# Products of neighbouring MLP units interleaved: a unit's first product stands between the fifth and sixth of its predecessor

## The chip, the cores and the metric

The kernel runs on one core of a Trainium2 chip. The metric is the device time of one execution in microseconds; the time before is the median of three runs. The core's engines are TensorE (PE), VectorE (DVE), ScalarE (ACT), GpSimd (POOL) and SyncE (SP); transfers are issued by SP, ACT and POOL.

## The reference

One layer of an encoder trunk on 512 tokens of width 2048, in float32:

```python
h = x + stick_breaking_mixer(rms_norm(x, norm_mix), w_qkv, w_o)   # 16 heads of 128
h = h + square(relu(rms_norm(h, norm_mlp) @ w1)) @ w2             # d_ff = 8192
return rms_norm(h, final_norm)
```

The change touches the MLP alone: `w1` is 2048 x 8192, `w2` is 8192 x 2048.

## The kernel before

**Precision.** Every float32 operand is split into two parts, hi (a cast to float32r) and lo (the remainder), and each product is made of three matmuls: hi·hi, hi·lo and lo·hi (`mm3`, lines 148 to 150).

**Units.** The MLP is done in 32 units (`units2`). Units 0 to 15 are the first stage: each makes 512 of the 8192 hidden columns. Units 16 to 31 are the second stage: pairs (c, q), c from 0 to 7, q from 0 to 1, that add 1024 hidden columns' share into one half of the 2048 output columns. Every unit splits its operands into 2 x 2 blocks and does them with seven block products instead of eight (a Strassen-like scheme). `ORDER` (line 385) lists the seven; an entry gives the activation mix on the left, the chain of weights on the right, the PSUM accumulator, and what is added to the chain afterwards:

```python
    ORDER = (
        ("11", "a", "x", (0, 1)),
        ("12", "c", "z", None),
        ("s1", "a", "y", "b"),
        ("s4", "b", "y", (0, 1)),
        ("s2", "a", "x", "c"),
        ("s3", "b", "x", None),
        ("22", "a", "x", None),
    )
```

Here the products are counted from 0 (11) to 6 (22). A chain is a pair of 0.5 MB buffers (tags `ra`, `rb`, `raw`) that holds one block of the weights and is changed in place: after product 0 another block is added to chain a by an accumulating transfer that POOL issues (`nc.gpsimd.dma_start(..., accum_op=ALU.add)`, line 432), after product 2 VectorE adds chain b into a (line 430), after product 3 POOL adds a block to b (line 432), after product 4 VectorE adds c into a.

**Splitting.** `split2` (line 416) goes through all products in order. For each half of a chain ScalarE casts it to hi (`whi`, line 426) and VectorE subtracts to get lo (`wlo`, line 427), into a pool of six buffers; a product uses four. Then come the additions above. It is called one product ahead of `run2`. It also issues the plain fetches (`fetch`, line 403, on SP's queue, line 408) of the next unit: chain a at product 0, c at product 4, b at product 5.

**Running.** `run2` (line 446) does a product's 48 (first stage, 256 columns) or 24 (second stage, 512 columns) matmuls, in two halves s = 0 and 1 with an accumulator bank each, then its evacuation: in the first stage copies, adds, ReLU and squares into tiles whose seven mixes are stored to DRAM (`a_dram`); in the second one VectorE instruction a half that adds the scaled product into a tile of h (line 537). Accumulator x is opened by product 0 and used again by 4, 5 and 6. Bank pool `acc_a` has four banks, two a unit. Small tasks in the list `side` (mixes, stores, reloads) are taken in turn, one after each half.

**Joints.** At the start of the MLP, transposes and mixes of the attention's output are still being done while product 0 of unit 0 runs; the pool `acc_b` then takes over PSUM banks that the transposes used. During unit 15 the mixes of c = 0 (`load_a(0, ...)`, 28 transfers of 256 KB) and the residual h (`load_h`, 16 of 256 KB, line 564) are loaded on SP's queue; in every q = 1 unit the mixes of the next c are queued, a name per product.

**Order.** The framework's scheduler orders each engine's instructions by program order as priority and by its own model of when each is ready; engines run their queues in that order and wait on semaphores.

Of the kernel before, what the change touches and what calls it, by code (L numbers as in the profile page):

```python
# [18 lines left out]
DF = 8192  # L19
# [3 lines left out]
W = 512  # L23
# [17 lines left out]
def trunk_kernel(  # L41
# [18 lines left out]
    acc_a = ctx.enter_context(tc.tile_pool(name="acc_a", bufs=4, space=PSUM))  # L60
# [91 lines left out]
    def ahead(i):  # L152
        split(i + 1)
        load(i + 4)
        split(i + 3)

    def run(p, pool, step=None, steps=1, behind=None):
        banks = [pool.tile([P, W], F32, name=f"acc{b}", tag="acc") for b in range(4)]
        ng = p.nk // G
        for g in range(ng):  # L160
            i = p.first_piece + g
            ahead(i)
            if behind and g == ng - 1:
                behind()
            parts = splits.pop(i)
            for b in range(4):
                if step is not None and b % (4 // steps) == 4 // steps - 1:
                    step()
                for j in range(G):
                    k = g * G + j  # L170
                    act = p.acts(k)
                    ca = slice(b * P, (b + 1) * P)
                    hi, lo = parts[j]
                    if p.weights_still:
                        a = (hi[:, ca], lo[:, ca])
                        m = act
                    else:
                        a = (act[0][:, ca], act[1][:, ca])
                        m = (hi, lo)
                    mm3(banks[b], a, m, k == 0, k == p.nk - 1)  # L180
                if g == ng - 1:
                    p.evac(b, banks[b])
# [39 lines left out]
    late = ([], [])  # L222
# [147 lines left out]
    def load_a(c, names):  # L370
        for name in names:
            for pl in range(2):
                parts = two(name)
                for i, t in enumerate(parts):
                    nc.sync.dma_start(f(t), a_dram[name, 2 * c + pl, i])
                mixed[name][c, pl] = parts
# [8 lines left out]
# [9 lines that stand above are left out]
# [16 lines left out]

    homes = {}
    units2 = []
    ready = {}
    done = {"split": 0}

    def split2(upto):

        while done["split"] < min(upto, 7 * len(units2)):
            i = done["split"]
            u, (_, chain, _, more) = units2[i // 7], ORDER[i % 7]  # L420
            parts = []
            for pc in range(2):
                raw = u.raw[chain, pc]
                hi = wp.tile([P, u.jn, u.width], F32R, name="whi", tag="w")
                lo = wp.tile([P, u.jn, u.width], F32R, name="wlo", tag="w")
                nc.scalar.copy(hi, raw)  # L426
                nc.vector.tensor_tensor(out=lo, in0=raw, in1=f(hi), op=ALU.subtract)  # L427
                parts.append((hi, lo))
                if more in ("b", "c"):
                    nc.vector.tensor_tensor(out=raw, in0=raw, in1=u.raw[more, pc], op=ALU.add)  # L430
                elif more:
                    nc.gpsimd.dma_start(raw, u.block(*more, pc), accum_op=ALU.add)  # L432
            ready[i] = parts
            done["split"] += 1
            nxt = units2[i // 7 + 1] if i // 7 + 1 < len(units2) else None
            if nxt:
                if i % 7 == 0:
                    nxt.fetch("a")
                elif i % 7 == 4:
                    nxt.fetch("c")  # L440
                elif i % 7 == 5:
                    nxt.fetch("b")

    side = []

    def run2(ui, still, pools, pace=1, only=range(7)):

        u = units2[ui]
        n = 256 if still else W
        for p in only:  # L450
            left, _, name, _ = ORDER[p]
            i = 7 * ui + p
            split2(i + 2)
            parts = ready.pop(i)
            fresh = (name, 0) not in u.acc
            for s in range(2):
                if fresh:
                    u.acc[name, s] = pools[name].tile([P, W], F32, name="acc2", tag="acc")
                ps = u.acc[name, s][:, 0:n]
                cs = slice(s * P, (s + 1) * P)  # L460
                for j in range(2 * u.jn):
                    hi, lo = (t[:, j % u.jn, :] for t in parts[j // u.jn])
                    ah, al = (t[:, j % 2, :] for t in mixed[left][u.key(j)])
                    start, stop = fresh and j == 0, j == 2 * u.jn - 1
                    if still:
                        mm3(ps, (hi[:, cs], lo[:, cs]), (ah, al), start, stop, True)
                    else:
                        mm3(ps, (ah[:, cs], al[:, cs]), (hi, lo), start, stop, True)
                u.evac(p, s, ps)
                for _ in range(pace[s] if isinstance(pace, tuple) else pace):  # L470
                    if side:
                        go = side.pop(0)
                        if go:
                            go()

    def evac_1(u):

# [82 lines left out]
    def load_h(ns):  # L560
        for n in ns:
            for tb in range(NT):
                hn[tb, n] = slot(F32, "h")
                nc.sync.dma_start(hn[tb, n], h_dram[tb, n])
# [36 lines left out]
    for grp in range(4):  # L601
        p = Panel([(w_qkv, 0, 2 * D + grp * W, W)], NK, x_acts, False, evac_v(grp))
        add_panel(p)
        qkv_panels.append(p)
        for pair in (2 * grp, 2 * grp + 1):
            p = Panel([(w_qkv, 0, pair * 256, 256), (w_qkv, 0, D + pair * 256, 256)], NK, x_acts, True, evac_qk(pair))
# [3 lines left out]
    for n in range(4):  # L610
        p = Panel([(w_o, 0, n * W, W)], NK, o_acts, False, evac_o(n))
        add_panel(p)
        o_panels.append(p)

    NC2 = DF // 1024

    def unit_1(u):
# [7 lines left out]
    def unit_2(c, q):  # L625
        def block(kh, nh, pc):
            r, cc = 512 * (2 * c + pc) + 256 * kh, 1024 * q + 512 * nh
            return w_2[r : r + 256, cc : cc + 512].rearrange("(j p) n -> p j n", p=P)
        x = Unit(block, 2, W, evac_2(c, q))
        x.key = lambda j: (c, j // 2)  # L630
        return x

    N1 = DF // 512
    units2.extend(unit_1(u) for u in range(N1))
    units2.extend(unit_2(c, q) for c in range(NC2) for q in range(2))

    with tc.tile_pool(name="att_ps", bufs=1, space=PSUM) as att_ps:

# [134 lines left out]
        for n in range(1, 4):  # L773
            for tb in range(NT):
                hn[tb, n] = slot(F32, "h")
                nc.scalar.dma_start(hn[tb, n], x[tb * P : (tb + 1) * P, n * W : (n + 1) * W])
            if n == 2:
                units2[0].fetch("a")
                units2[0].fetch("b")
            run(o_panels[n], acc_a, turn, 2, behind=first_weights if n == 3 else None)  # L780
        side.extend(late[0] + late[1])
        run2(0, True, {"x": acc_a}, pace=(len(late[0]), 4), only=range(1))
        side.extend(turns)

    with tc.tile_pool(name="acc_b", bufs=4, space=PSUM) as acc_b:
        pools = {"x": acc_a, "y": acc_b, "z": acc_b}
        run2(0, True, pools, pace=4, only=range(1, 2))
        token_scales()
        run2(0, True, pools, pace=3, only=range(2, 7))
        for u in range(1, N1):  # L790
            if u < N1 - 1:
                run2(u, True, pools)

        steps = [lambda: load_a(0, ("11", "12")), lambda: load_h((0, 1)), lambda: load_a(0, ("s1", "s4")),
                 lambda: load_a(0, ("s2", "s3")), lambda: load_a(0, ("22",)), lambda: load_h((2,)), lambda: load_h((3,))]
        for p, load_more in enumerate(steps):
            run2(N1 - 1, True, pools, only=range(p, p + 1))
            load_more()
        for c in range(NC2):
            for q in range(2):  # L800
                if q and c < NC2 - 1:
                    for name, *_ in ORDER:
                        side.extend([lambda name=name, c=c: load_a(c + 1, (name,)), None])
                elif c == NC2 - 1 and q == 0:
                    side.append(load_gain)
                run2(N1 + 2 * c + q, False, pools)


# [30 lines left out]
```

## Time and profile before

| | |
|---|---|
| median of 3 runs | 2120.33 us (2117.99 to 2120.54) |
| profiled execution | 2123.21 us, span 2121.2 us |
| mean granted TensorE clock | 0.994 |
| TensorE, VectorE, ScalarE, POOL busy | 98%, 66%, 46%, 9% |
| transfers | 376.35 MB, mean 177 GB/s |

The span is the time from the first to the last instruction of the profiled execution; the rest of its time lies around it. A matmul's end is modelled and overlaps the start of the next, so a busy TensorE is not one at its peak; the spacing of matmul starts is the better measure.

### The profile page before, as it was taken

Reading aid. Unit: us, or ns where it says so; the run is one execution under the profiler, and the core shown is the slowest. Engines: PE = TensorE matmul, PEld = TensorE weight load, DVE = VectorE, ACT = ScalarE, POOL = GpSimd, SP = SyncE. Lnnn points to the kernel's source line nnn. Section 1 sums busy time; section 2 is a strip of 40 time slices with the busy share of each in tenths; the row PEclk is TensorE's granted clock in tenths of the full one; section 3 lists DMA queues with packets and bytes.
Section 4 is the critical chain, followed back from the end, with each engine's and each line's share of the span. In section 5 each row is a group of like instructions: output and inputs, shape, how many; then the busy total and the mean of one; then the engine's idle time right before and its main releaser. Section 6 shows DMA issues by size and latency. Waiting matters only on the chain.

```text
span 2121.2 us, 30309 instructions
## 1 busy us (share of the span) xinstructions
PE 2071.3 (98%) x11766; PEld 1814.9 (86%) x11766; DVE 1389.6 (66%) x1629; ACT 971.5 (46%) x1344; POOL 194.1 (9%) x217
## 2 busy tenths in 40 slices
PE   9999999999999998999999999998999999999997
PEld 7888888888888888999999999997777877877886
DVE  7354453553552457777777777776777877877887
ACT  6343343342442345656666665664333333333344
POOL 0000000000000000110110111111010111101222
PEclk9999999999999999999999999999999999999999
DMA  6222322222235354878879879899988779778654
GB/s 199 90 80 81 97 75 87 90 80 81 89 96 192 130 139 115 213 201 240 222 198 237 229 204 222 240 244 350 323 258 250 184 234 256 188 219 250 149 147 119
DMA packets 257055, 376.35 MB, mean 177 GB/s; under 512 B 16768, under 2 KB 131472, under 8 KB 256912
## 3 DMA queue, kind: packets, MB, share of 16 engines
q1 hardware_dynamic: 199344, 295.76, 41.3%
q0 software_dynamic: 51232, 67.13, 20.0%
q10 hardware_dynamic: 6336, 11.54, 1.6%
q8 instruction: 92, 1.51, 0.3%
q14 instruction: 51, 0.42, 0.1%
HBM read 307.25 MB, written 67.11 MB: 176 GB/s over the span
## 4 chain that ended last, share of the span: by engine, by line
PE 46%; issue 40%; POOL 5%; DMA 5%; DVE 2%; ACT 1%; POOLq 0%; SPq 0%; ACTq 0%
PE acc L149 14%; PE acc L150 14%; PE acc L148 14%; DMA rb<-w_dram 3%; POOL rb L432 3%; POOL ra L432 3%; DVE wlo L427 1%; DMA ra<-w_dram 1%; PE at L725 1%; ACT whi L426 1%; DMA s3h<-as 1%; PE z L149 0%; PE ot L149 0%; PE z L150 0%; PE ot L150 0%
## 5 line engine op out<-in xcount | busy, mean ns | idle before, releaser
L426 ACT CAST whi<-ra 128x1024 fp32r<-128x1024 f32 x256 | 268.2, 1050 | 323.8 <-PE acc L149 274.6
L427 DVE TENSOR_TENSOR wlo<-ra,whi 128x1024 fp32r<-128x1024 f32 x256 | 314.6, 1229 | 150.5 <-ACT whi L426 146.2
L141 DVE TENSOR_TENSOR wlo<-raw,whi 128x1024 fp32r<-128x1024 f32 (+1 forms) x129 | 156.6, 1215 | 264.4 <-ACT whi L140 264.2
L140 ACT CAST whi<-raw 128x1024 fp32r<-128x1024 f32 (+1 forms) x129 | 134.8, 1046 | 262.1 <-PE acc L149 248.1
L426 ACT CAST whi<-rb 128x1024 fp32r<-128x1024 f32 x128 | 134.5, 1051 | 161.4 <-PE acc L149 96.0
L427 DVE TENSOR_TENSOR wlo<-rb,whi 128x1024 fp32r<-128x1024 f32 x128 | 158.7, 1241 | 65.6 <-ACT whi L426 64.1
L148 PE MATMUL acc<-thi,whi 128*128 128x512 f32 x512 | 201.1, 393 | 0.0
L150 PE MATMUL acc<-thi,wlo 128*128 128x512 f32 x512 | 199.8, 390 | 0.0
L149 PE MATMUL acc<-tlo,whi 128*128 128x512 f32 x512 | 199.5, 390 | 0.0
L537 DVE SCALAR_TENSOR_TENSOR h<-acc,stat,h 128x512 f32<-128x512 f32 x224 | 166.8, 745 | 9.0 <-PE acc L150 9.0
L432 POOL DMA_DIRECT2D ra<-w_dram x64 | 79.4, 1240 | 791.9 <-DVE wlo L427 693.1
L432 POOL DMA_DIRECT2D rb<-w_dram x64 | 79.5, 1249 | 457.2 <-DVE wlo L427 410.8
L150 PEld LDWEIGHTS acc<-thi,wlo 128*128 128x128 f32 x512 | 96.1, 188 | 20.5
L148 PEld LDWEIGHTS acc<-thi,whi 128*128 128x128 f32 x512 | 96.2, 188 | 19.2
L149 PEld LDWEIGHTS acc<-tlo,whi 128*128 128x128 f32 x512 | 96.2, 188 | 19.0
L148 PE MATMUL acc<-whi,thi 128*128 128x512 f32 x256 | 100.3, 397 | 0.9 <-ACT whi L140 0.9
L148 PE MATMUL acc<-whi,ohi 128*128 128x512 f32 x256 | 101.2, 395 | 0.0
L149 PE MATMUL acc<-wlo,thi 128*128 128x512 f32 x256 | 100.2, 391 | 0.3 <-DVE wlo L141 0.3
L150 PE MATMUL acc<-whi,olo 128*128 128x512 f32 x256 | 100.2, 391 | 0.0
L150 PE MATMUL acc<-whi,tlo 128*128 128x512 f32 x256 | 100.0, 391 | 0.0
L149 PE MATMUL acc<-wlo,ohi 128*128 128x512 f32 x256 | 99.8, 390 | 0.0
L426 ACT CAST whi<-raw 128x1024 fp32r<-128x1024 f32 x64 | 67.4, 1052 | 64.1 <-PE acc L149 62.2
(234 smaller groups left out, 5800.0 us busy)
## 6 DMA issues: line engine op xcount, KB each, us to landing
raw<-w_qkv_dram SPq DMA_DIRECT2D x130, 256.0 KB, 2.9
ra<-w_dram SPq DMA_DIRECT2D x64, 512.0 KB, 5.1
rb<-w_dram SPq DMA_DIRECT2D x64, 512.0 KB, 5.7
raw<-w_dram SPq DMA_DIRECT2D x64, 512.0 KB, 6.1
ra<-w_dram POOLq DMA_DIRECT2D x64, 512.0 KB, 7.4
rb<-w_dram POOLq DMA_DIRECT2D x64, 512.0 KB, 7.9
raw<-w_o_dram SPq DMA_DIRECT2D x32, 512.0 KB, 3.8
raw<-w_qkv_dram SPq DMA_DIRECT2D x31, 512.0 KB, 3.9
```

The source lines that it names most:

```text
L140: nc.scalar.copy(hi[:, js, :], raw[:, js, :])
L141: nc.vector.tensor_tensor(out=lo[:, js, :], in0=raw[:, js, :], in1=f(hi[:, js, :]), op=ALU.subtract)
L148: nc.tensor.matmul(ps, lhsT=a[0], rhs=b[0], start=start, stop=False, skip_group_check=goes_on)
L149: nc.tensor.matmul(ps, lhsT=a[0], rhs=b[1], start=False, stop=False, skip_group_check=goes_on)
L150: nc.tensor.matmul(ps, lhsT=a[1], rhs=b[0], start=False, stop=stop, skip_group_check=goes_on)
L426: nc.scalar.copy(hi, raw)
L427: nc.vector.tensor_tensor(out=lo, in0=raw, in1=f(hi), op=ALU.subtract)
L432: nc.gpsimd.dma_start(raw, u.block(*more, pc), accum_op=ALU.add)
L537: nc.vector.scalar_tensor_tensor(out=t, in0=ps, scalar=by, in1=t, op0=ALU.mult, op1=ALU.add)
L725: nc.tensor.transpose(out=ps[:, kb * P : (kb + 1) * P], in_=beta[:, kb * P : (kb + 1) * P], identity=ident)
```

## The change

The order of the products becomes a list, `order`, of pairs (unit, product). It begins with product 0 of units 0 and 1; then each unit has its products 1 to 4, product 0 of the next unit (from unit 1 on), and its products 5 and 6. `split2` and `run2` go through this list. The fetches of c and b stay at products 4 and 5; the fetch of chain a moves from product 0 (for the next unit) to product 6 (for the unit after next), and unit 1's chain a is fetched before the MLP begins. The reloads of mixes and h are hung on products of the list by `afterwards`. No arithmetic is added or removed.

```diff
--- before.py
+++ after.py
@@ -410,14 +410,16 @@
 
     homes = {}
     units2 = []
+    order = []
     ready = {}
-    done = {"split": 0}
+    done = {"split": 0, "run": 0}
 
     def split2(upto):
 
-        while done["split"] < min(upto, 7 * len(units2)):
+        while done["split"] < min(upto, len(order)):
             i = done["split"]
-            u, (_, chain, _, more) = units2[i // 7], ORDER[i % 7]
+            n, p = order[i]
+            u, (_, chain, _, more) = units2[n], ORDER[p]
             parts = []
             for pc in range(2):
                 raw = u.raw[chain, pc]
@@ -432,24 +434,21 @@
                     nc.gpsimd.dma_start(raw, u.block(*more, pc), accum_op=ALU.add)
             ready[i] = parts
             done["split"] += 1
-            nxt = units2[i // 7 + 1] if i // 7 + 1 < len(units2) else None
-            if nxt:
-                if i % 7 == 0:
-                    nxt.fetch("a")
-                elif i % 7 == 4:
-                    nxt.fetch("c")
-                elif i % 7 == 5:
-                    nxt.fetch("b")
+            for number, chain, ahead_by in ((4, "c", 1), (5, "b", 1), (6, "a", 2)):
+                if p == number and n + ahead_by < len(units2):
+                    units2[n + ahead_by].fetch(chain)
 
     side = []
 
-    def run2(ui, still, pools, pace=1, only=range(7)):
-
-        u = units2[ui]
-        n = 256 if still else W
-        for p in only:
+    def run2(count, pools, pace=1):
+
+        for _ in range(count):
+            i = done["run"]
+            done["run"] += 1
+            un, p = order[i]
+            u, still = units2[un], un < N1
+            n = 256 if still else W
             left, _, name, _ = ORDER[p]
-            i = 7 * ui + p
             split2(i + 2)
             parts = ready.pop(i)
             fresh = (name, 0) not in u.acc
@@ -472,6 +471,10 @@
                         go = side.pop(0)
                         if go:
                             go()
+            if (un, p) in afterwards:
+                afterwards[un, p]()
+
+    afterwards = {}
 
     def evac_1(u):
 
@@ -612,6 +615,7 @@
         add_panel(p)
         o_panels.append(p)
 
+    N1 = DF // 512
     NC2 = DF // 1024
 
     def unit_1(u):
@@ -630,9 +634,15 @@
         x.key = lambda j: (c, j // 2)
         return x
 
-    N1 = DF // 512
     units2.extend(unit_1(u) for u in range(N1))
     units2.extend(unit_2(c, q) for c in range(NC2) for q in range(2))
+
+    order.extend([(0, 0), (1, 0)])
+    for un in range(len(units2)):
+        order.extend((un, p) for p in range(1, 5))
+        if 0 < un < len(units2) - 1:
+            order.append((un + 1, 0))
+        order.extend((un, p) for p in range(5, 7))
 
     with tc.tile_pool(name="att_ps", bufs=1, space=PSUM) as att_ps:
 
@@ -777,33 +787,38 @@
             if n == 2:
                 units2[0].fetch("a")
                 units2[0].fetch("b")
+                units2[1].fetch("a")
             run(o_panels[n], acc_a, turn, 2, behind=first_weights if n == 3 else None)
         side.extend(late[0] + late[1])
-        run2(0, True, {"x": acc_a}, pace=(len(late[0]), 4), only=range(1))
+        run2(1, {"x": acc_a}, pace=(len(late[0]), 4))
         side.extend(turns)
+        run2(1, {"x": acc_a}, pace=1)
 
     with tc.tile_pool(name="acc_b", bufs=4, space=PSUM) as acc_b:
         pools = {"x": acc_a, "y": acc_b, "z": acc_b}
-        run2(0, True, pools, pace=4, only=range(1, 2))
+
+
+        def begin(names, ns):
+            def go():
+                load_h(ns)
+                load_a(0, names)
+            return go
+
+        last = N1 - 1
+        for p, names, ns in ((0, ("11",), ()), (1, ("12",), (0,)), (2, ("s1",), (1,)), (3, ("s4", "s2"), ()),
+                             (4, ("s3", "22"), ()), (5, (), (2,)), (6, (), (3,))):
+            afterwards[last, p] = begin(names, ns)
+        for c in range(1, NC2):
+            def queue_loads(c=c):
+                for name, *_ in ORDER:
+                    side.extend([lambda name=name: load_a(c, (name,)), None])
+            afterwards[N1 + 2 * (c - 1), 5] = queue_loads
+        afterwards[N1 + 2 * NC2 - 3, 5] = load_gain
+
+        run2(1, pools, pace=3)
         token_scales()
-        run2(0, True, pools, pace=3, only=range(2, 7))
-        for u in range(1, N1):
-            if u < N1 - 1:
-                run2(u, True, pools)
-
-        steps = [lambda: load_a(0, ("11", "12")), lambda: load_h((0, 1)), lambda: load_a(0, ("s1", "s4")),
-                 lambda: load_a(0, ("s2", "s3")), lambda: load_a(0, ("22",)), lambda: load_h((2,)), lambda: load_h((3,))]
-        for p, load_more in enumerate(steps):
-            run2(N1 - 1, True, pools, only=range(p, p + 1))
-            load_more()
-        for c in range(NC2):
-            for q in range(2):
-                if q and c < NC2 - 1:
-                    for name, *_ in ORDER:
-                        side.extend([lambda name=name, c=c: load_a(c + 1, (name,)), None])
-                elif c == NC2 - 1 and q == 0:
-                    side.append(load_gain)
-                run2(N1 + 2 * c + q, False, pools)
+        run2(5, pools, pace=3)
+        run2(len(order) - done["run"], pools)
 
 
 def kernel(x, norm_mix, norm_mlp, final_norm, sb_w_qkv, sb_w_o, mlp_w1, mlp_w2, **unused):
```

## Rows read from the trace of the kernel before

**Rows 1.** Page, part 1: by engine, busy us, share of the span, instructions.

```profile
PE 2071.3 (98%) x11766; PEld 1814.9 (86%) x11766; DVE 1389.6 (66%) x1629; ACT 971.5 (46%) x1344; POOL 194.1 (9%) x217
```

**Rows 2.** Windows, two undisturbed stretches; the first line names the columns.

```profile
core 0: us, PE busy (x) PEld busy (x) DVE busy (x) ACT busy (x) POOL busy (x), PEclk, DMA share, GB/s
...
1588.56:1610.32 21.76, 21.76 (x97) 18.02 (x96) 18.40 (x20) 8.42 (x8) 3.58 (x3) 1.00 0.80 196
...
1093.14:1162.26 69.12, 69.12 (x579) 69.12 (x577) 54.43 (x62) 42.06 (x60) 9.01 (x7) 1.00 0.84 208
```

**Rows 3.** Windows, the MLP in five stretches; columns as in rows 2.

```profile
792.02:848.52 56.50, 48.10 (x353) 46.80 (x352) 42.55 (x62) 33.80 (x56) 3.83 (x3) 0.91 0.47 121
848.52:1416.77 568.25, 566.36 (x4706) 564.90 (x4705) 430.96 (x491) 352.11 (x504) 71.95 (x56) 1.00 0.85 221
1416.77:1548.67 131.90, 121.91 (x674) 104.19 (x673) 96.07 (x107) 57.51 (x71) 14.64 (x12) 0.99 1.06 336
1548.67:2030.60 481.93, 467.18 (x2018) 379.51 (x2016) 369.92 (x385) 175.85 (x169) 65.35 (x52) 0.99 0.79 218
2030.60:2110.50 79.90, 77.38 (x336) 62.28 (x335) 67.67 (x83) 39.21 (x60) 26.96 (x19) 1.00 0.47 105
```

**Rows 4.** Waits, 1548.67 to 2030.6 us: total us, times, longest.

```profile
ACT whi L426 <- DMA rb<-w_dram: 29.8, 12, 4.0
...
ACT whi L426 <- DMA ra<-w_dram: 27.9, 10, 3.8
...
PE acc L149 <- DVE wlo L427: 8.3, 11, 0.8
...
PE acc L148 <- ACT whi L426: 4.3, 8, 1.0
...
PE acc L148 <- DVE h L537: 2.0, 3, 1.2
```

**Rows 5.** Timeline, one late b; start, us, instruction, idle before it.

```profile
1606.34 1.20 POOL L432 DMA_DIRECT2D rb<-w_dram  x1 [1.56 <-DVE wlo L427]
...
1617.23 1.05 ACT L426 CAST whi<-rb 128x1024 fp32r<-128x1024 f32 x1 [2.91 <-DMA rb<-w_dram]
...
1619.60 0.50 PE L149 MATMUL acc<-wlo,s3h 128*128 128x512 f32 x1 [0.77 <-DVE wlo L427]
```

**Rows 6.** Timeline, one late a, from issue to TensorE.

```profile
1630.25 1.20 POOL L432 DMA_DIRECT2D ra<-w_dram  x1 [2.44 <-DMA s3h<-as]
...
1641.26 1.04 ACT L426 CAST whi<-ra 128x1024 fp32r<-128x1024 f32 x1 [3.32 <-DMA ra<-w_dram]
...
1642.35 0.51 PE L148 MATMUL acc<-whi,s1h 128*128 128x512 f32 x1 [0.92 <-ACT whi L426]
...
1643.61 0.52 PE L149 MATMUL acc<-wlo,s1h 128*128 128x512 f32 x1 [0.75 <-DVE wlo L427]
```

**Rows 7.** Window around the wait of rows 6; columns as in rows 2.

```profile
1640.00:1660.00 20.00, 18.33 (x73) 14.46 (x72) 15.87 (x18) 7.26 (x7) 2.39 (x2) 0.91 0.48 102
```

**Rows 8.** Landing: L432, then L408 (1548 to 2031 us), then L564.

```profile
DMA to landing us min/median/max: 6.0/6.7/11.4
...
DMA to landing us min/median/max: 3.6/4.9/9.6
...
DMA to landing us min/median/max: 5.3/5.8/8.5
```

**Rows 9.** Timeline of TensorE in unit 0, then a window.

```profile
794.90 1.04 PE L311 MATMUL ht<-ident,hs 128*128 128x128 f32 x8
...
802.72 0.39 PE L148 MATMUL acc<-12h,whi 128*128 128x256 f32 x1 [3.04 <-ACT hin L318]
...
818.67 0.39 PE L148 MATMUL acc<-s2h,whi 128*128 128x256 f32 x1 [1.40 <-ACT whi L426]
...
820.00:840.00 20.00, 17.64 (x117) 17.20 (x118) 13.41 (x17) 8.74 (x15) 1.19 (x1) 0.83 0.71 165
```

## The prediction

> **What bounds the kernel now.** I read the page first. TensorE is busy for 98% of the span, VectorE for 66% [rows 1]: this is a TensorE kernel, and a reordering can only return the time in which TensorE stands still or runs slowly. So the second question is how fast it goes when nothing disturbs it. Two undisturbed stretches, read with the windows, answer it [rows 2]: in the second MLP stage four products (96 matmuls of 512 columns) take 21.76 us, 226.7 ns each, 5.44 us a product; in the first stage twelve products (576 matmuls of 256 columns) take 69.12 us, 120 ns each, 5.76 us a product. The counts there are a few higher because matmuls that begin before a border overlap it. Both stretches ran at granted clock 1.00.
>
> The third view is the MLP cut into five stretches [rows 3], each held against its products at that pace. Unit 0: 56.50 us for 40.32 of products and about 1.6 of transposes (an estimate: 16 of them, of which 8 take 1.04 us to their modelled end [rows 9]), so 14.6 lost. Units 1 to 14: 568.25 against 98 x 5.76 = 564.48, 3.8 lost. Units 15 to 17, where the stages meet: 131.90 against 40.32 + 76.16, 15.4 lost. Units 18 to 29: 481.93 against 84 x 5.44 = 456.96, 25.0 lost. Units 30 and 31: 79.90 and some 0.4 behind the last border, against 76.16, 4.2 lost. Together 63 us: nothing inside the MLP can gain more.
>
> The fourth view says who is late. In units 18 to 29 TensorE waits only for wlo, whi and h, 14.6 us in 22 waits [rows 4]; but ScalarE, which makes whi, waits 29.8 us in 12 waits for a DMA into rb and 27.9 us in 10 for one into ra, none longer than 4.0. These are POOL's accumulating DMAs: product 3 (s4) leaves one on chain b, needed by product 5 (s3); product 0 (11) leaves one on chain a, needed by product 2 (s1). There is one product between each pair. The chain can be followed once for b [rows 5]: POOL issues the second half at 1606.34, ScalarE idles 2.91 us until 1617.23, VectorE makes wlo, TensorE resumes at 1619.60. And once for a [rows 6]: issue at 1630.25, cast at 1641.26 after 3.32 us, TensorE waits 0.92 and 0.75.
>
> The 25.0 us are more than the 14.6 of waits. A wait is counted from the modelled end of the matmul before, 0.39 us after its start though the next could have started 0.227 after, so each hides about 0.16: 22 of them, 3.6. The rest, about 6.8, is the clock: in the 20 us around the wait of [rows 6] the mean granted clock is 0.91 [rows 7]: 3.6 us were spent at the lower level, 1.2 GHz, and did 1.8 us of work. These losses go when the waits that come before them go.
>
> **The change part by part.** It adds and removes no matmul, cast, subtraction or transfer; every term is a move.
>
> (1) Product 0 of unit n+1 goes between products 4 and 5 of unit n. Chain b's accumulation then has two products to land in instead of one: 5.44 us more. Longest wait on rb: 4.0, so all 12 waits end, with 1.4 us to spare. Chain a's has three instead of one, 10.88 more against a longest wait of 3.8. What was late now lands in the shadow of the moved product 0 and of products 5, 6 and 1. Next in line is the cast-and-subtract of each half, which waits for a free weight buffer; that pattern is in the undisturbed products too and costs them nothing, and VectorE's 369.92 us of work [rows 3] would then fill 81% of 457. Taken: 24 of 25.0 us, 1 us left for a late wlo here and there.
>
> (2) Units 1 to 14 lose their 3.8 to the same two products. Taken: 3.5.
>
> (3) Units 15 to 17 lose to it as well, but here the engines' DMA share is 1.06 at 336 GB/s [rows 3], since h and the first two reloads of activations arrive. The change spreads them a little: the reloads of c = 0 and h go from 7 products to 10, and from the first of them to the last of c = 1 there are 23 products instead of 21. By bounds: 0 if the transfers set the pace there, 15.4 if all vanishes; the waits seen elsewhere fit within the added 5 to 11 us, so I take 11. The h block that the moved product 0 of unit 16 adds into is loaded behind product 1 of unit 15, 3.5 products (about 20 us) ahead; its transfers took at most 8.5 [rows 8].
>
> (4) Unit 0: TensorE waits 3.04 us for hin at the change of PSUM pools and then for weights and split activations [rows 9], with a clock of 0.83 between 820 and 840. VectorE has a backlog of transposed activations. Now product 0 of unit 1, 5.76 us whose activations are already there, stands in front of that: it hides the 3.04 and gives VectorE time to catch up. By bounds 3.0 to 14.6; taken 8.6, since the scheduler lets s2 in before its weights are split here [rows 9], and that need not vanish.
>
> (5) Units 30 and 31: taken 1.7 of 4.2, the rest hangs on the evacuations of the end.
>
> (6) Moves that are hidden. The fetch of a for unit n+2 waits for the same free buffer as before and has five products. That of c keeps its place. That of b has three products (16.3 us) instead of four before VectorE adds it into a; fetches landed within 9.6 us in units 18 to 29 [rows 8]. If that cover went, VectorE, in order, would hold the evacuations and subtractions queued behind the add. PSUM: two units' x accumulators are open at once, four banks, all that acc_a has; the third unit's opens after the first's is closed. SP's queue is passed by the same transfers, POOL's by the same four a unit, but the b and a accumulations are now two products apart (10.9 us), then five. The 48 of units 18 to 29 landed 6.0 to 11.4 us after issue [rows 8], so they can touch.
>
> The Trainium skill, DMA: Bandwidth & Descriptors, section Anatomy of one DMA — SWDGE (gpsimd) path, fits a GpSimd DMA at 2.0 us and its bytes at 436 GB/s: 3.2 us (an estimate by that page) for 0.5 MB. By it the transfer would be long there when the cast wants it, and the change would return (4) and (5) alone. The trace does not agree: the fastest took 6.0 [rows 8].
>
> Sum: 24 + 3.5 + 11 + 8.6 + 1.7 = 48.8. The profiled execution took 2123.21 (span 2121.2), so 2074.4; the median of the runs is 2.9 lower, 2071.5. I keep 1.5 for waits not foreseen and predict **2073**.
>
> **Rivals.** (A) Contention. The accumulations now follow each other closely and still meet the reloads, and an accumulation that lands over 1.4 us later than the worst now puts b's wait back. By ScalarE's waits about half of the 25.0 us is b's [rows 4]. If that half stays and the joint of the stages keeps all: 48.8 - 12.5 - 11, a gain of 25, time 2095. For it: the share of 1.06; against: units 18 to 29 move 218 GB/s on average [rows 3], and only the bursts are full.
>
> The Trainium skill, same page, section Issuing engines are not separate DMA queues, says that POOL's and SP's transfers share the 16 engines; nothing in the change takes that away, and it is the ground of this rival.
>
> (B) Hidden anyway: the accumulation is as late as the order lets it be, because the transfers themselves set the pace. Then only (4) and (5) are gained: 2110. Against it: an average share of 0.79 [rows 3], and undisturbed units beside disturbed ones.
>
> (C) The change does not do what it says: engine order is chosen by the scheduler from modelled readiness, and it could put product 5 first again wherever it believes b to be there. Time 2120, within 0.2%. Against it: program order is its priority, and both are ready.
>
> (D) Slower: b's fetch. It has 16.3 us; if SP held it until it landed 18 us after its buffer came free, VectorE's add would stop the in-order queue for 1.6 us in each of 30 units, 48 us, and the gain would be gone; 3 us each would give 2073 + 90 = 2163. Landings of at most 9.6 speak against it.
>
> **How the numbers follow.** Forecast 0.75, (A) 0.15, (B) 0.04, (C) 0.03, (D) 0.03. A difference of 0.2% (4 us) is about what a measurement of this kernel can tell. Forecast, (A) and (B) are all faster by more: 0.94; same 0.03; slower 0.03. The lowest sensible time is all 63 us gone, 2057; the forecast's own bounds, from (3) and (4), are 2061 to 2086. The range reaches towards (A): 2061 to 2092.
>
> **What would show it.** Right: in the second stage ScalarE's waits for rb and ra fall from 57.7 us in units 18 to 29 to a few, units take 38.1 us, the clock stays at 1.00 in all of them, and landing times stay at 6 to 12 us. In unit 0 the 3.04 us wait for hin is gone. Span about 2072. Wrong: waits of VectorE's adds on rb (D), s3 still late in the odd units (A), product 0 of the next unit behind product 5 on TensorE (C), or products in another order than the one written, in more units than the first.

## The result, and the profile after

The changed kernel takes 2084.59 us (median of 4 runs, 2082.44 to 2085.52) against 2120.30 before (median of 4 as well): ratio 0.9833, interval 0.9815 to 0.985. It is 1.7% faster; 2073 was forecast, in a range of 2061 to 2092. The profiled execution took 2084.27 us, span 2082.5.

The page's busy times, as in [rows 1]:

```profile
PE 2054.1 (99%) x11766; PEld 1810.4 (87%) x11766; DVE 1382.6 (66%) x1629; ACT 971.3 (47%) x1344; POOL 192.5 (9%) x217
```

The windows of the changed kernel, columns as in [rows 2]. The borders are starts of product 2 (s1) of units 1, 15, 18 and 30, so a stretch holds other products than its counterpart in [rows 3].

```profile
793.64:855.89 62.25, 56.08 (x449) 54.95 (x448) 50.20 (x71) 40.00 (x65) 5.13 (x4) 0.97 0.56 136
855.89:1420.47 564.58, 564.58 (x4706) 564.53 (x4705) 425.69 (x491) 350.42 (x504) 71.98 (x56) 1.00 0.84 224
1420.47:1544.87 124.40, 118.74 (x627) 102.34 (x625) 95.82 (x107) 55.30 (x66) 14.53 (x12) 0.99 1.03 320
1544.87:2002.66 457.79, 457.55 (x2017) 378.23 (x2016) 369.17 (x386) 177.49 (x169) 64.34 (x52) 1.00 0.83 235
2002.66:2082.50 79.84, 67.20 (x289) 53.33 (x287) 63.65 (x87) 39.43 (x66) 25.36 (x18) 0.97 0.47 119
```

Held against the undisturbed pace: the first stretch has 9 products of 5.76 and the 1.6 of transposes, and loses 8.8; the second 98 products, loses 0.1; the joint has 5 of 5.76 and 16 of 5.44, 115.84, and loses 8.6; the fourth has 84 of 5.44, 456.96, and loses 0.8; the last (from 2002.66 to 2072.18, where at the pace the last matmul would be over) 12 of 5.44, and loses 4.2. All stretches of experiments below are worked out so. The mean clock of the fourth stretch is 1.00; before it was 0.99 [rows 3], and 0.91 in the 20 us around a wait [rows 7].

ScalarE's waits in the fourth stretch (total us, times, longest). The two lines on rb and ra of [rows 4] are gone; of transfers only chain c's fetch and one reload are still waited for. The fetch that is late is unit 19's, and the 0.8 us are lost there, at product 1 of unit 19:

```profile
ACT whi L428 <- PE acc L149: 276.1, 164, 3.4
...
ACT whi L428 <- DMA raw<-w_dram: 4.2, 2, 3.9
...
ACT whi L428 <- DMA s2h<-as: 0.3, 1, 0.3
```

Landing there, of the accumulations (L434) and of the plain fetches (L408), to set against [rows 8]. Their medians are higher than before (6.7 and 4.9 us), and neither ScalarE nor VectorE waits for an accumulation:

```profile
DMA to landing us min/median/max: 6.0/9.0/12.3
...
DMA to landing us min/median/max: 3.6/8.0/14.8
```

TensorE and ScalarE in unit 0 (timeline; the number in brackets is the idle time before), and the window of 820 to 840. The wait for hin of [rows 9] is gone. Product s2 still runs ahead of s4, and s4, which goes on in the accumulator of s1, waits until ScalarE has copied y out of it:

```profile
822.20 0.58 PE L150 MATMUL acc<-s2h,wlo 128*128 128x256 f32 x1 [0.41 <-DVE wlo L429]
827.00 0.38 PE L148 MATMUL acc<-s2h,whi 128*128 128x256 f32 x1 [1.01 <-ACT whi L428]
...
832.76 0.38 PE L148 MATMUL acc<-s4h,whi 128*128 128x256 f32 x1 [1.85 <-ACT y L507]
...
832.35 0.36 ACT L507 COPY y<-acc 128x256 f32<-128x256 f32 x1
...
820.00:840.00 20.00, 15.27 (x108) 14.35 (x109) 15.43 (x22) 11.03 (x19) 2.14 (x2) 0.91 0.67 159
```

### The profile page after: what moved, and what is told of

It reads as the page before. It is cut to its first block, busy times and chain, and to the rows that moved or that the text cites. A ratio compares the mean times of both kernels' runs of the same rounds, so it can differ in the third digit from the quotient of the medians.

```text
span 2082.5 us, 30381 instructions
## 1 busy us (share of the span) xinstructions
PE 2054.1 (99%) x11766; PEld 1810.4 (87%) x11766; DVE 1382.6 (66%) x1629; ACT 971.3 (47%) x1344; POOL 192.5 (9%) x217
## 4 chain that ended last, share of the span: by engine, by line
PE 93%; DMA 3%; DVE 2%; ACT 1%; issue 1%; ACTq 0%; SPq 0%; POOLq 0%
PE acc L148 30%; PE acc L150 30%; PE acc L149 30%; PE at L735 1%; DVE wlo L429 1%; ACT whi L428 1%; DMA raw<-w_dram 1%; DMA s3h<-as 1%; PE z L149 0%; PE ot L149 0%; PE z L150 0%; PE ot L150 0%; DMA raw<-w_qkv_dram 0%; PE z L148 0%; PE ot L148 0%
## 5 line engine op out<-in xcount | busy, mean ns | idle before, releaser
L540 DVE SCALAR_TENSOR_TENSOR h<-acc,stat,h 128x512 f32<-128x512 f32 x224 | 166.9, 746 | 10.5 <-PE acc L150 10.5
L434 POOL DMA_DIRECT2D rb<-w_dram x64 | 79.5, 1248 | 765.8 <-DVE wlo L429 638.4
L434 POOL DMA_DIRECT2D ra<-w_dram x64 | 79.4, 1240 | 435.5 <-DVE wlo L429 401.3
L150 PEld LDWEIGHTS acc<-thi,wlo 128*128 128x128 f32 x512 | 96.1, 188 | 20.6
L429 DVE TENSOR_TENSOR wlo<-raw,whi 128x1024 fp32r<-128x1024 f32 x64 | 78.4, 1225 | 48.8 <-ACT whi L428 47.3
```

The costliest lines, as they stand in the source:

```text
L150: nc.tensor.matmul(ps, lhsT=a[1], rhs=b[0], start=False, stop=stop, skip_group_check=goes_on)
L540: nc.vector.scalar_tensor_tensor(out=t, in0=ps, scalar=by, in1=t, op0=ALU.mult, op1=ALU.add)
```

## The experiments

**Theory:** the old order gave an accumulation one product to land in; two products are more than it needs, also in the densest traffic. What the change leaves (22.5 us) hangs on other things: the order in unit 0, the loads of the joint (units 15 to 17), VectorE at the end. **Rivals:** contention, so that the distance matters little; a gain from something that comes along, such as the spread reloads.

Losses by stretch in us, from the first matmul of each product of the profiled execution; times are medians, ratios are to the kernel before, run beside each.

| kernel | time | ratio, interval | unit 0 | 1-14 | joint | 18-29 | 30-31 |
|---|---|---|---|---|---|---|---|
| before | 2120.30 | | 14.6 | 3.8 | 15.4 | 25.0 | 4.2 |
| after | 2084.59 | 0.9833 (0.9815-0.985) | 8.8 | 0.1 | 8.6 | 0.8 | 4.2 |
| again (after) | 2086.08 | 0.9841 (0.9827-0.9854) | 11.1 | 0.1 | 10.0 | 0.2 | 4.1 |
| x56 | 2111.86 | 0.9958 (0.9943-0.9973) | 10.4 | 2.1 | 20.6 | 12.5 | 4.9 |
| x65 | 2106.41 | 0.9936 (0.9921-0.995) | 12.0 | 5.5 | 17.7 | 6.5 | 4.3 |
| x34 | 2092.09 | 0.9864 (0.985-0.9878) | 12.0 | 0.1 | 14.8 | 0.0 | 4.2 |
| nore | 2095.14 | 0.9878 (0.9863-0.9893) | 14.5 | 3.0 | 12.1 | 0.0 | 4.2 |
| nore_after | 2092.67 | 0.9866 (0.9852-0.988) | 7.7 | 0.1 | 17.1 | 0.0 | 4.3 |
| slots | 2079.40 | 0.9811 (0.9795-0.9828) | 2.9 | 0.0 | 10.5 | 0.0 | 4.1 |
| loads | 2082.48 | 0.982 (0.9806-0.9834) | 10.5 | 0.1 | 6.0 | 1.3 | 4.1 |
| joint | 2078.48 | 0.98 (0.9786-0.9814) | 3.2 | 0.0 | 9.2 | 0.0 | 4.0 |
| joint2 | 2075.90 | 0.9793 (0.978-0.9807) | 3.0 | 0.0 | 5.5 | 1.9 | 4.0 |
| port | 2075.33 | 0.9789 (0.9776-0.9803) | 3.0 | 0.0 | 4.5 | 3.7 | 3.5 |

The repeat of the changed kernel sets what a difference between two single profiles means: 2.3 us in unit 0, 1.4 at the joint, 0.6 in units 18 to 29.

The outputs of x65, nore and nore_after are not the reference's; they are run for their times alone.

**x56: product 0 of the next unit between products 5 and 6.** Chain b's accumulation has one product to land in, as before the change; chain a's has two.

```diff
-        order.extend((un, p) for p in range(1, 5))
+        order.extend((un, p) for p in range(1, 6))
         if 0 < un < len(units2) - 1:
             order.append((un + 1, 0))
-        order.extend((un, p) for p in range(5, 7))
+        order.append((un, 6))
```

> Product 0 of the next unit stands between products 5 and 6 instead of 4 and 5. Theory (time to land): b's accumulation has one product again, a's two. Units 18 to 29 lose some 11 us, all of it at s3 and nothing at s1; the time is 2095 to 2100. Rival (any foreign product inside a unit helps, by giving evacuations and VectorE room): no loss comes back, 2083 to 2088.

**x65: products in the order 1, 2, 3, 4, 6, 5, then product 0 of the next unit.** Chain a's accumulation has one product to land in, as before the change; chain b's has two. (Two keys of first-stage stores, swapped to fit, are left out of the diff.)

```diff
-        order.extend((un, p) for p in range(1, 5))
+        order.extend((un, p) for p in ((1, 2, 3, 4, 6, 5) if un < len(units2) - 1 else range(1, 7)))
         if 0 < un < len(units2) - 1:
             order.append((un + 1, 0))
-        order.extend((un, p) for p in range(5, 7))
```

> Products 5 and 6 change places and product 0 of the next unit stands behind both (the accumulators' contents at these two products are then others, so the output is not the reference's). b's accumulation has two products, a's one. Theory: units 18 to 29 lose some 14 us, all of it at s1 and nothing at s3; 2098 to 2103. Rival (foreign product): as no product of another unit stands inside a unit, all of the loss comes back, 2109 to 2115 (the start of the MLP keeps its gain).

ScalarE's waits in units 18 to 29, first x56, then x65:

```profile
ACT whi L428 <- DMA rb<-w_dram: 31.3, 10, 3.8
```

```profile
ACT whi L428 <- DMA ra<-w_dram: 26.8, 11, 3.6
```

Each chain waits again exactly where its second product was taken away, and the other does not: s3 of odd units in x56, s1 of even units in x65. The mechanism stands. Both kernels have the changed kernel's spread reloads, and x56 has a product of another unit inside each unit, so neither of these is what gained here. The sizes: units 18 to 29 lose 12.5 us in x56, near the some 11 expected, and 6.5 in x65, where some 14 were expected. Both times (2111.86 and 2106.41) lie above what the theory gave, since 20.6 and 17.7 us are lost at the joint, against 8.6 in the changed kernel; in x65 units 1 to 14 lose 5.5 besides. Why the joint loses so much in these two was not followed up.

**x34: product 0 between products 3 and 4.** Chain b's accumulation has two products to land in, chain a's four.

```diff
-        order.extend((un, p) for p in range(1, 5))
+        order.extend((un, p) for p in range(1, 4))
         if 0 < un < len(units2) - 1:
             order.append((un + 1, 0))
-        order.extend((un, p) for p in range(5, 7))
+        order.extend((un, p) for p in range(4, 7))
```

> The next unit's product 0 between products 3 and 4: b's accumulation still has two products to land in, a's has four instead of three. Theory (two products are enough): the same as the changed kernel, 2081 to 2088, units 18 to 29 lose under 2 us. Rival A (contention sets how late they are): the accumulation of a and that of b are issued within one product of each other, both land later and units 18 to 29 lose over 5 us: time 2088 to 2096.

Units 18 to 29 and the landing of the accumulations:

```profile
1553.81:2010.77 456.96, 456.96 (x2017) 378.50 (x2016) 368.99 (x385) 177.60 (x169) 65.43 (x52) 1.00 0.82 230
...
DMA to landing us min/median/max: 5.9/8.1/13.8
```

84 products in 456.96 us: not a tenth of a microsecond is lost. The accumulation that landed after 13.8 is one of chain a, which has four products; on chain b, which has two, none took over 11.3 us. Two products are enough. The time is 2092 all the same, inside the range that was expected of contention, but for another reason: the joint loses 14.8 and unit 0 12.0. Of the 14.8, 8.5 stand in unit 15, where the scheduler sets 14 matmuls of the moved product 0 ahead of s4, and 4.9 at s3 of unit 16, which was not followed up.

**nore: the kernel before without the reloads of the mixes for c = 1 to 7; nore_after: the changed kernel without them.**

```diff
         for name in names:
             for pl in range(2):
+                if c:
+                    mixed[name][c, pl] = mixed[name][0, pl]
+                    continue
```

> The kernel before, but the second stage reloads no activation mixes after those of c = 0 (c = 0's stand in for all, so the output is not the reference's). Theory (the accumulations are late because the reloads' bursts slow them): units 18 to 29 lose under 5 us instead of 25.0, accumulations land in 6 to 8 us, time 2092 to 2100. Rival (one product is too short for an accumulation even on quiet DMA engines): over 15 us stay lost in units 18 to 29, 2108 to 2120.

> The changed kernel without the reloads of the activation mixes for c from 1 to 7 (c = 0's are used throughout, so the products of later units differ from the reference's). Theory (the accumulations land later but nobody waits for them any more): accumulations land in 5.9 to 7 us again, units 18 to 29 lose 0 us instead of 0.8, and the time falls by no more than 1 to 5 us, to 2079 to 2084, all of that at the joint. Rival (the reloads still cost the changed kernel time): under 2078.

Landing of the accumulations in units 18 to 29, first nore, then nore_after:

```profile
DMA to landing us min/median/max: 5.9/6.1/6.8
```

```profile
DMA to landing us min/median/max: 5.9/6.3/9.5
```

With the old order and no reloads no accumulation is late: the 25.0 us are two things together, the distance of one product and the reloads, among which an accumulation takes up to 11.4 us [rows 8] instead of 6.8. The Trainium skill, DMA: Bandwidth & Descriptors, section Issuing engines are not separate DMA queues, says that transfers which POOL and SP issue run on the same DMA engines; these two rows agree. In the changed kernel taking the reloads away gains 0.8 us there and no more. Its whole time went up, against the expectation: without the reloads ScalarE issues the loads of the final gain at 1492 instead of 1947, and they hold its queue and then TensorE (timeline):

```profile
1492.65 8.65 ACTq L575 DMA_DIRECT2D gain<-g_fin_dram  x4
...
1502.51 1.22 PE L148 MATMUL acc<-whi,22h 128*128 128x512 f32 x2 [6.26 <-ACT whi L431]
```

TensorE loses 8.2 us at that product. The rest of the joint loses 8.9, in the same places as in the changed kernel: the later reloads cost nothing there either.

**slots: the first stage's tiles y1, u2 and c21 in places of their own.** In the changed kernel the copy of y comes at 832.35, and s4, which goes on in that accumulator, behind it. The three tiles are moved together, so the run doesn't tell them apart.

```diff
-                got[name] = slot(F32, name).rearrange("p (i q) -> p i q", q=256)
+                own = {"y1": first, "c21": rstd_bc}
+                t = own[name] if name in own else spare.tile([P, W], F32, name="u2") if name == "u2" else slot(F32, name)
+                got[name] = t.rearrange("p (i q) -> p i q", q=256)
...
+        spare = ctx.enter_context(tc.tile_pool(name="spare", bufs=1))
```

> The changed kernel with the first-stage evacuation tiles y1, u2 and c21 in buffers of their own instead of in the shared pool of 72. Theory (what is still lost in unit 0 and in units 15 and 16 comes from evacuations that wait for a free buffer, so that the scheduler puts s2 ahead of s4): s4 runs before s2 in unit 0, nearly so in unit 15; 6 to 9 us less than the changed kernel, 2075 to 2079. Rival (unit 0 is VectorE's backlog of mixes, units 15 and 16 are the transfers): within 2 us of the changed kernel, 2083 to 2087.

```profile
815.67 0.37 ACT L509 COPY first<-acc 128x256 f32<-128x256 f32 x1 [2.09 <-PE acc L150]
...
818.30 0.38 PE L150 MATMUL acc<-s4h,wlo 128*128 128x256 f32 x1 [0.28 <-DVE wlo L429]
```

The copy now follows s1 at 815.67, s4 is back in its place, and unit 0 loses 2.9 us. The joint's sum is no smaller (10.5), but it stands elsewhere: unit 15, where s4 is back in its place, too, loses nothing, and units 16 and 17 lose all of it. The same kernel shows what is late there: on SP's queue the second half of chain b's fetch stands behind eight reloads and two stores and is issued at 1458.12, and VectorE's add waits for each half:

```profile
1450.15 0.38 SPq L408 DMA_DIRECT2D rb<-w_dram  x1
...
1458.12 0.38 SPq L408 DMA_DIRECT2D rb<-w_dram  x1
...
1456.17 1.22 DVE L432 TENSOR_TENSOR ra<-ra,rb 128x1024 f32<-128x1024 f32 x1 [2.87 <-DMA rb<-w_dram]
...
1464.05 1.23 DVE L432 TENSOR_TENSOR ra<-ra,rb 128x1024 f32<-128x1024 f32 x1 [2.40 <-DMA rb<-w_dram]
```

**joint, joint2, loads: the reloads of c = 0 and h spread over eleven places.** joint and joint2 have the edit of slots too, loads has not. joint2 is shown; joint has s3, 22 and the h block 2 at (last, 6), (N1, 1) and (N1, 2).

```diff
-        for p, names, ns in ((0, ("11",), ()), (1, ("12",), (0,)), (2, ("s1",), (1,)), (3, ("s4", "s2"), ()),
-                             (4, ("s3", "22"), ()), (5, (), (2,)), (6, (), (3,))):
-            afterwards[last, p] = begin(names, ns)
+        for at, names, ns in (((last, 0), ("11",), ()), ((last - 1, 5), ("12",), ()), ((last, 1), (), (0,)),
+                              ((last, 2), ("s1",), ()), ((last, 3), (), (1,)), ((last, 4), ("s4",), ()),
+                              ((last, 5), ("s2",), ()), ((last, 6), (), (2,)), ((N1, 1), ("s3",), ()),
+                              ((N1, 2), ("22",), ()), ((N1, 4), (), (3,))):
+            afterwards[at] = begin(names, ns)
```

> The changed kernel with the three tiles of slots in places of their own and, besides, the reloads of c = 0 and h spread over eleven places of the order, one name or one h block at a place, up to product 4 of unit 16, so that no two reloads stand on SP's queue ahead of unit 16's fetches of c and b at once. Theory (the joint loses its time because those fetches queue behind the reloads): the joint falls from the 10.5 us lost in slots to under 5, VectorE's adds no longer wait for rb there, time 2071 to 2076. Rival (the transfers of the joint are limited by their bytes, whatever their order): the joint keeps 8 to 10 us, time 2077 to 2081. Second rival (h or mixes now come too late for units 16 and 17): waits for h or the mixes appear there, time above 2080.

> The changed kernel with the spread reloads of joint alone; the three tiles stay in the common pool. Theory: unit 0 loses 8.8 us as in the changed kernel; at the joint the swap of s2 and s4 stays, but the fetches' waits go, so the joint falls from 8.6 us to 3 to 6: time 2079 to 2082. If the two causes are not independent (the swap is what the late fetch shows itself through), the joint falls under 3: time 2076 to 2079. Rival (order of the loads without effect): 2083 to 2086.

> joint with the h block of unit 17 loaded three places earlier (behind product 6 of unit 15) and the reloads of s3 and 22 one place later each. Theory (what joint kept is one wait of VectorE for that h block, which held the casts' partner subtractions queued behind it): the 8.2 us at s3 of unit 16 go, the joint loses 1 to 3 us, time 2069 to 2074. Rival (transfers at the joint are limited by their bytes, so the wait moves to the next consumer): the joint keeps over 6 us, time 2076 to 2080.

In joint the waits for rb are gone, but the joint loses 9.2 and the time is 2078.48, both inside the first rival's range and not the theory's; h now comes late: issued at 1471.86, waited for by VectorE, which holds the wlo behind it, for which TensorE waits:

```profile
1471.86 2.19 SPq L569 DMA_DIRECT2D h<-h  x4
...
1482.28 0.75 DVE L542 SCALAR_TENSOR_TENSOR h<-acc,stat,h 128x512 f32<-128x512 f32 x1 [7.48 <-DMA h<-h]
...
1484.21 0.79 PE L149 MATMUL acc<-wlo,s3h 128*128 128x512 f32 x1 [6.26 <-DVE wlo L429]
```

In joint2 that wait is gone too, and TensorE waits for the mix of s3 itself:

```profile
1479.73 0.47 PE L148 MATMUL acc<-whi,s3h 128*128 128x512 f32 x1 [0.76 <-DMA s3h<-as]
...
1481.61 0.79 PE L150 MATMUL acc<-whi,s3l 128*128 128x512 f32 x1 [1.17 <-DMA s3l<-as]
```

The joint loses 10.5, 9.2 and 5.5 us in slots, joint and joint2: the place on SP's queue decides who is late, but 5.5 lies between theory and rival, and the wait went from b to h to s3, as the rival has it. Whether the bytes set the rest (the joint's DMA share is 1.03 in joint2, as in the changed kernel) is not shown. loads came in at 2082.48, 3.6 us below the repeat of the changed kernel, on another chip and with intervals that touch; alone it is inconclusive. joint2 is 10.2 us below the repeat on the same chip.

**port: joint2 with the final gain multiplied on VectorE instead of POOL.** The 4.2 us of units 30 and 31 stood in every kernel.

```diff
-            nc.gpsimd.tensor_tensor(out=t, in0=t, in1=g_bc[n], op=ALU.mult)
+            nc.vector.tensor_tensor(out=t, in0=t, in1=g_bc[n], op=ALU.mult)
```

> joint2 with the twelve multiplications of finished h blocks by the final gain on VectorE instead of POOL. Theory (the 4.2 us of units 30 and 31, which no order of the products changed, come from VectorE's two-input instructions lasting up to 2.31 us instead of 1.22 while POOL multiplies h by the gain): those instructions last 1.2 us throughout, units 30 and 31 lose under 2.5 us, time 1 to 3 us below joint2. Rival (VectorE is the bound there, 12 times 0.65 us more work costs more than the slowing): units 30 and 31 lose over 5 us, time above joint2.

> The changed kernel once more, beside the two others on the same chip: 2082 to 2086 us, and by stretches within 1 us of its first profile at the joint and in units 18 to 29, if differences of that size between kernels mean anything.

The changed kernel, then port (timeline):

```profile
2005.09 1.89 POOL L552 TENSOR_TENSOR h<-h,gain 128x512 f32<-128x512 f32 x1 [0.34 <-ACT junk L550]
...
2005.75 2.31 DVE L429 TENSOR_TENSOR wlo<-rb,whi 128x1024 fp32r<-128x1024 f32 x1
```

```profile
1997.83 1.22 DVE L429 TENSOR_TENSOR wlo<-rb,whi 128x1024 fp32r<-128x1024 f32 x1
1998.96 0.69 DVE L554 TENSOR_TENSOR h<-h,gain 128x512 f32<-128x512 f32 x1
```

Without POOL's multiplications no such subtraction lasts over 1.23 us. But the stretch loses 3.5 instead of 4.0, which is less than two profiles differ by, and the time is joint2's: either the slowing cost TensorE little, or VectorE's added work costs as much. The cause of the 4.2 us is not settled by this. What joint2 and port lose in units 18 to 29 (1.9 and 3.7) stands at product 1 of unit 19, as in the changed kernel, behind a late fetch of chain c (waits of 5.0 and 5.6 us).

## Why the prediction was right, and where its size was off

**(1), units 18 to 29: 24 forecast, 24.2 came** (25.0 to 0.8; 0.2 in the repeat), with the clock at 1.00. The waits on rb and ra did not merely shrink, they are gone. x56 and x65 show that it is the distance of each chain. The forecast's margin was real and thin: a landing could grow by 1.4 us over the worst of 11.4 before b waits again, and it grew by 0.9, to 12.3. The accumulations stayed close to the forecast's 6 to 12 us, but their median rose from 6.7 to 9.0, and the plain fetches took up to 14.8 instead of 9.6: some of rival A's contention came, and the distance hid it. The 14.8 is a fetch of chain c; those of b, which have 16.3 us, landed within 11.9, so D stayed away here, too. Chain c, which the prediction passed over since it keeps its place, is the one that is late, once.

**(2), units 1 to 14: 3.5 forecast, 3.7 came.**

**(3), the joint: 11 forecast, 6.8 came** (5.4 by the repeat). This step failed in size, and in its reason. It took the whole loss of 15.4 to be of the kind that the added distance covers, and 11 of it to go. By the matmul starts of the kernel before, 5.1 us stand in unit 15, where s2 runs ahead of s4 and TensorE then waits for the copy of u out of an accumulator:

```profile
1435.23 0.39 PE L148 MATMUL acc<-s2h,whi 128*128 128x256 f32 x1 [1.02 <-ACT whi L426]
...
1450.61 0.39 PE L148 MATMUL acc<-s3h,whi 128*128 128x256 f32 x1 [2.71 <-ACT u L509]
```

The distance does nothing for these: in the changed kernel unit 15 loses 6.3, in the same way as unit 0. The copy of y comes late, s4 follows it, and s3 waits for the copy of u. Products in another order than the one written, in more units than the first, are a sign that the prediction had named for being wrong:

```profile
1427.41 0.39 PE L148 MATMUL acc<-s2h,whi 128*128 128x256 f32 x1 [1.02 <-ACT whi L428]
...
1433.70 0.64 ACT L507 COPY y<-acc 128x256 f32<-128x256 f32 x2
...
1434.30 0.28 PE L148 MATMUL acc<-s4h,whi 128*128 128x256 f32 x1
...
1449.38 0.39 PE L148 MATMUL acc<-s3h,whi 128*128 128x256 f32 x1 [1.18 <-ACT u L512]
```

In units 16 and 17, 10.3 us were lost before and 2.3 are now; there the distance did most of what was forecast. Nearly all of the 2.3 stands at s4 of unit 16: a plain fetch of chain b is held back on SP's in-order queue behind reloads, ScalarE waits 3.38 us for it, VectorE's add 2.82, and TensorE then 1.93 for work that ScalarE does behind that cast. Rival D's mechanism (b's fetch late, VectorE's add holding its queue) stands at this one place, most clearly in slots:

```profile
1456.94 0.38 SPq L408 DMA_DIRECT2D rb<-w_dram  x1
...
1458.88 0.32 SPq L375 DMA_DIRECT2D s3h<-as  x1
...
1464.83 0.38 SPq L408 DMA_DIRECT2D rb<-w_dram  x1
...
1470.87 1.05 ACT L428 CAST whi<-rb 128x1024 fp32r<-128x1024 f32 x1 [3.38 <-DMA rb<-w_dram]
...
1473.99 0.47 PE L148 MATMUL acc<-whi,s4h 128*128 128x512 f32 x1 [1.93 <-ACT c L490]
```

**(4), unit 0: 8.6 forecast, 5.8 came** (3.5 by the repeat). The wait for hin went, as forecast; s2 ahead of s4 remained and was only named as a doubt. Its cause, evacuations that wait for tiles of the common pool, was missed; slots shows that it is worth 6 us.

**(5), units 30 and 31: 1.7 forecast, nothing came**, in any order of products.

**The sum:** the MLP gave back 40.4 us (62.9 to 22.5) of 48.8. The rest of the miss of 11.6: the MLP began 1.6 us later (793.6 against 792.0; 792.5 to 793.6 in the other kernels), and the profiled execution of before, 2.9 above its median, was followed by one 0.3 below, 3.2; less the 1.5 kept for waits: 8.4 + 1.6 + 3.2 - 1.5 = 11.7. The prediction's own upper bound of 2086 does not follow from its terms: (3) at 0 and (4) at 3.0 are 16.6 us less gain, which from 2071.5 gives 2088; the measured time lies below either.

## What to carry to other kernels

When a transfer that is issued after one product and needed a product later is late only in dense traffic, moving independent work in between can do as much as taking the other traffic away (here 0.8 us are left in units 18 to 29 by the one, none by the other), and it leaves no work out: the order keeps its gain even while the transfers get slower. Cost such a move stretch by stretch and unit by unit, and look in each for what is late there; a wait of the same length at a joint can have another cause (a tile that isn't free, an in-order queue). Where a profiled execution stands off its median, carry the difference as a bound, not as a correction.

## What the runs showed of the hardware

An accumulating transfer of 0.5 MB took 6.0 to 11.4 us among the reloads in the old order and 5.9 to 6.8 without them (nore); in the new order it took 6.0 to 12.3, in a stretch that lost 0.8 us of 458, and 5.9 to 9.5 without them (nore_after).

A subtraction of VectorE with two inputs in SBUF took 2.31 us instead of 1.22 beside POOL's multiplication: POOL ended at 2006.98, VectorE at 2008.06, 1.08 later, nearly as if it had begun when POOL was done. The Trainium skill, SBUF — State Buffer, section SBUF: two separate sides, says that VectorE and GpSimd share a port pair that the first of them holds for its whole instruction; the trace agrees, and so does port, where no such pair stands and 1.23 is the longest.
